# Input projections as seven products for eight, with q, k and v taken through DRAM

## The chip, the core and the metric

The kernel runs on one core of one Trainium2 chip. A core has the matrix engine (PE in the profile, with PEld for its weight loads), the vector engine (DVE), the scalar engine (ACT), GpSimd (POOL) and an engine that here issues nearly all transfers (SP). They run side by side and wait for each other through semaphores. The metric is device time in microseconds of one execution; three runs of the kernel before are shown.

## What is computed

Two layers of a decoder trunk, on 1024 tokens of 1024 columns in f32. Each layer normalises its input, applies gain and shift, and multiplies by one combined weight matrix. Four mLSTM heads and four retention heads of 256 columns work on the result in chunks of the sequence; their gated output is multiplied by a second matrix and added to the input.

```python
for l in range(DEPTH):
    ada = c_act @ w_ada[l] + b_ada[l]
    shift, scale, gate = jnp.split(ada, 3, axis=-1)
    h = rmsnorm(x, norm_g[l]) * (1.0 + scale[:, None, :]) + shift[:, None, :]
    p = h @ w_in[l]
    mq, mk, mv, mo, mz, mi, mf, rq, rk, rv, rz = split_cols(p)
    qk = jax.nn.silu(causal_dwconv(jnp.concatenate([mq, mk], axis=-1), conv_w[l], conv_b[l]))
    ...
    cell = mlstm_chunkwise(mq_c, mk_c, mv, mi + b_igate[l], mf + b_fgate[l])
    y_m = jax.nn.sigmoid(mo) * head_layernorm(cell, gn_m[l], 4) * jax.nn.silu(mz)
    ret = retention_chunkwise(rotary(rq, positions), rotary(rk, positions), rv)
    y_r = head_layernorm(ret, gn_r[l], 4) * jax.nn.silu(rz)
    x = x + gate[:, None, :] * (jnp.concatenate([y_m, y_r], axis=-1) @ w_out[l])
return rmsnorm(x, final_g)
```

The product `h @ w_in[l]` has 1024 rows (tokens), an inner length of 1024 and 9224 columns: q, k, v of eight heads, z of eight heads, o of the four mLSTM heads (1024 columns for each kind and each group of four heads), and eight columns for the input and forget gates.

## The kernel before

**Numbers.** Every f32 operand of a large matmul is split into a high part (ACT casts it to fp32r, L621) and a low part (another engine subtracts, L622; POOL where nothing else is said). `mm3` (L144) makes one product out of three matmuls: high by high, high by low, low by high.

**Tiles.** The normalised input is kept transposed, `hT[k][half]`: eight row tiles `k` of the inner length by two halves of 512 tokens, high and low, 32 tiles of a pool of 62 (`b`). A projection of q, k, z or o takes a block of 128 weight columns as the stationary operand and streams 512 tokens: two halves by eight `k` by three matmuls, 48 matmuls of 512 columns (`proj_units`, L363). The values of a head take 128 tokens as the stationary operand and stream the 256 weight columns: 192 matmuls of 256 columns (`v_path`, L579). PSUM has two pools of four banks: `pp` for projections and `pa` for the rest.

**Order.** PE's order is the program's own: `run_units` (L140) walks a generator of work units, and after each unit `tick` runs the pieces of attention and other side work that are due (`launch`, with a delay in units). The other engines' instructions are put in order by a scheduler at build time; each engine then works strictly in that order. A layer goes: first blocks of z and o of head 0 while the input is being normalised; the values of head 0 together with the eight gate columns (`v0_units`, L434), the rest of head 0's z and o; then for each head z and o blocks, q, k (`qk_ml`, L681, with convolution and SiLU in `conv_silu`, L630; `qk_ret`, L701, with the rotary sums L707 to L717) and v, with the attention of the head before running under them; at last the out projection (`out_units`, L985), whose weights and inputs `OutLoads` (L955) fetches. The mLSTM heads come first (0 to 3), then the retention heads (4 to 7).

**What stays in SBUF.** q and k of a head are split and stay in tiles of pool `b`, v is scaled and split straight out of PSUM (L607, L608). k also goes to DRAM (`kdr`) and back in rows for the state update. The normalised output of a head goes to DRAM (`ndr`, L919), as the gates do (`gdr`).

**Side work.** `rotary_tables` (L374) makes sine and cosine once, under head 1; `ada_columns_later` (L270) makes gain and shift of the second layer under head 4 and after it; `gate_cols` or `gate_rows` (L304, L284) make the gate of the layer from head 5 on.

Of the kernel before, what the change touches and what calls it, by code (L numbers as in the profile page):

```python
# [19 lines left out]
P = 128  # L20
# [15 lines left out]
BIG = 1e30  # L36
WHOLE = (0, 3)
# [43 lines left out]
def tile_hybrid_trunk(ctx, tc, x, xt, c, positions, w_ada, b_ada, norm_g, w_in, conv_w, conv_b,  # L81
# [8 lines left out]
    big = ctx.enter_context(tc.tile_pool(name="big", bufs=62))  # L90
# [53 lines left out]
    def mm3(o, lt, rt, start, stop):  # L144
        PE.matmul(o, lt[0], rt[0], start=start, stop=False)  # L145
        PE.matmul(o, lt[0], rt[1], start=False, stop=False)  # L146
        PE.matmul(o, lt[1], rt[0], start=False, stop=stop)  # L147
# [21 lines left out]
    kdr = [[[dpool.tile([HD, HALF], F32, name=f"kdr{l}_{h}_{i}") for i in range(2)] for h in range(8)]  # L169
           for l in range(DEPTH)]  # L170
# [83 lines left out]
    def ada_rows(l, c0, accs):  # L254
        acc = bt()
        accs.append(acc)
        prev = None
        for k in range(KT + 1):
            raw = None
            if k < KT:  # L260
                raw = wt("raw", 512, 4)
                Q.dma_start(raw, w_ada[l, k * P:(k + 1) * P, c0:c0 + 512])
# [21 lines left out]
    def gate_rows(l, res):  # L284
        for half in range(2):
            accs = []
            yield from ada_rows(l, 2 * D + half * 512, accs)
            brow = wt("th", 512, 5)
# [5 lines left out]
            a2 = (wt("wH", 512, 6, F32R), wt("wL", 512, 6, F32R))  # L294
# [35 lines left out]
    def norm_evac(l, pt, k, on_act=False):  # L330
        hf = wt("acc", 512, 4)
# [16 lines left out]
    def split_w(raw, n, eng=G):  # L348
        wH, wL = wt("wH", 512, 6, F32R), wt("wL", 512, 6, F32R)
# [24 lines left out]
    def rotary_tables():  # L374
        c1, c2, c3 = two_pi_split()
        tiles = [wt("g", 512, 6) for _ in range(3)]
        ang, turn, tmp, rnd, a1, pos = (t[:, i * CH:(i + 1) * CH] for t in tiles for i in range(2))
        a2 = ang
        for n in range(4):
# [13 lines left out]
            for src, cc in ((a1, c2), (a2, c1), (a1, c1)):  # L393
                V.tensor_scalar(tmp, src, cc, None, ALU.mult)
                V.tensor_scalar(rnd, tmp, MAG_I, -MAG_I, ALU.add, ALU.add)
                yield 1
# [16 lines left out]
    def v0_gates(l):  # L413
# [5 lines left out]
    def v0_raw(l, k):  # L419
        raw = wt("raw", 512, 4)[:, 0:HD]  # L420
        Q.dma_start(raw, w_in[l, k * P:(k + 1) * P, OFF_MV:OFF_MV + HD])
        return raw

    def v0_split(gr, raw, k):
        wH, wL = bt(F32R, HD + 8), bt(F32R, HD + 8)
        split_to((wH[:, HD:], wL[:, HD:]), gr[:, k * 8:(k + 1) * 8])
        split_to((wH[:, 0:HD], wL[:, 0:HD]), raw)
        return wH, wL

    def load_v0(l):  # L430
        gr = v0_gates(l)
        return [v0_split(gr, v0_raw(l, k), k) for k in range(KT)]

    def v0_units(l, w, hT, vraw, pgs):  # L434
        g8 = wt("g8", 8 * 36, 1)
        V.memset(g8, 0.0)
        for t in range(8):
            if t % 2 == 0:
                vraw.append(bt())
# [105 lines left out]
    def z_evac(res, m, store=None):  # L545
        def evac(half, pz):
# [5 lines left out]
            if store is not None:  # L552
                Q.dma_start(store[m][half], g)
# [849 lines left out]
```

## Time and profile before

| | us |
|---|---|
| runs (three): median, lowest, highest | 2300.58, 2298.8, 2301.35 |
| profiled execution: span from first to last instruction | 2298.7 |
| out projection of layer 0, about | 1030 to 1170 |
| last out projection, about | 2120 to 2298 |

Times in rows are from the start of the span. A row of a group names the line, the engine, the operation, output and inputs by the program's tile names, shapes and the count, then the summed busy time in us, the mean ns of one, and the idle time of the engine in front of them with what ended most of it. A row of a waits view names the engine and the instruction that waited, what it waited for, us in total, times, and the longest. In a table of stretches each engine has its busy us and its instructions (x), in the order PE, PEld, DVE, ACT, POOL; then the granted clock, the share of the DMA engines and GB/s. Matmuls overlap in the pipe, so the mean ns of a matmul is longer than the distance between two starts.

### The profile page before, as it was taken

The page shows a single profiled execution, that of the slowest core. Times are in us where ns is not written, and L with a number is a line of the kernel's source. Part 1 is how long each engine was busy: PE and PEld are TensorE (multiplying, and loading weights), DVE is VectorE, ACT ScalarE, POOL GpSimd, SP SyncE. Part 2 cuts the span into 40 slices and gives each one's busy share as a digit, 9 for nine tenths or more (in the row PEclk, how much of TensorE's full clock was granted, in tenths as well). Part 3 has the DMA queues.
Part 4 walks back from the last instruction along what each step waited for, and adds up shares of the span by engine and source line. Part 5 has one row for each costly group of instructions (what it writes and reads, how often), then busy time and mean ns, then how long its engine had stood idle before and what let it go on. Part 6 is the DMA issues. An engine that isn't in the chain of part 4 may idle for free. (4 is left out here: it accounts for less than half of the span.)

```text
span 2298.7 us, 34322 instructions
## 1 busy us (share of the span) xinstructions
PE 2269.4 (99%) x12411; PEld 1953.7 (85%) x12411; DVE 1338.7 (58%) x2821; ACT 926.5 (40%) x1785; POOL 827.5 (36%) x820
## 2 busy tenths in 40 slices
PE   7999999999999999999999999999999999999998
PEld 5888888889988888988888889888898898988886
DVE  7467688556555555585435676555564545556563
ACT  7535433444332323343544454444343323234442
POOL 0343333333333334224562434333334334341313
PEclk9999999999999999999999999999999999999999
DMA  8333333324433533476532323233223233436674
GB/s 258 80 69 94 83 80 82 83 70 115 124 110 87 149 96 79 126 254 212 169 105 67 84 71 82 77 77 79 68 71 98 74 91 88 124 84 205 184 242 125
DMA packets 360246, 259.45 MB, mean 113 GB/s; under 512 B 113266, under 2 KB 297338, under 8 KB 360076
## 3 DMA queue, kind: packets, MB, share of 16 engines
q1 hardware_dynamic: 359932, 257.00, 39.8%
q8 instruction: 97, 1.59, 0.3%
q14 instruction: 73, 0.60, 0.1%
q10 hardware_dynamic: 144, 0.26, 0.0%
HBM read 201.57 MB, written 55.61 MB: 112 GB/s over the span
## 5 line engine op out<-in xcount | busy, mean ns | idle before, releaser
L145 PE MATMUL pp<-b,wH 128*128 128x512 f32 x1824 | 719.6, 395 | 0.0
L146 PE MATMUL pp<-b,wH 128*128 128x512 f32 x1824 | 718.6, 394 | 0.0
L147 PE MATMUL pp<-b,wL 128*128 128x512 f32 x1824 | 717.6, 393 | 0.0
L622 POOL TENSOR_TENSOR wL<-raw,wH 128x512 fp32r<-128x512 f32 x338 | 453.9, 1351 | 542.3 <-ACT wH L621 478.7
L147 PEld LDWEIGHTS pp<-b,wL 128*128 128x128 f32 x1824 | 342.5, 188 | 80.4
L145 PEld LDWEIGHTS pp<-b,wH 128*128 128x128 f32 x1824 | 342.7, 188 | 73.1 <-DVE g L550 0.3
L146 PEld LDWEIGHTS pp<-b,wH 128*128 128x128 f32 x1824 | 342.5, 188 | 72.1 <-issue 0.2
L621 ACT CAST wH<-raw 128x512 fp32r<-128x512 f32 x402 | 245.7, 616 | 310.8 <-PE pp L146 109.9
L145 PE MATMUL pp<-wH,b 128*128 128x256 f32 (+1 forms) x1024 | 303.0, 296 | 0.0
L147 PE MATMUL pp<-wH,b 128*128 128x256 f32 (+1 forms) x1024 | 301.9, 295 | 0.0
L146 PE MATMUL pp<-wL,b 128*128 128x256 f32 (+1 forms) x1024 | 301.9, 295 | 0.0
L622 POOL TENSOR_TENSOR b<-acc,b 128x256 fp32r<-128x256 f32 (+1 forms) x192 | 176.6, 939 | 299.0 <-ACT b L621 287.7
L146 PEld LDWEIGHTS pp<-wL,b 128*128 128x128 f32 x1024 | 192.9, 188 | 5.8
L145 PEld LDWEIGHTS pp<-wH,b 128*128 128x128 f32 x1024 | 192.4, 188 | 6.0 <-DVE g L550 0.3
L147 PEld LDWEIGHTS pp<-wH,b 128*128 128x128 f32 x1024 | 192.7, 188 | 5.7
L639 DVE SCALAR_TENSOR_TENSOR acc<-pp,cols,acc 128x511 f32<-128x511 f32 (+2 forms) x192 | 142.4, 742 | 40.7 <-ACT acc L634 38.8
L621 ACT CAST b<-acc 128x256 fp32r<-128x256 f32 (+1 forms) x192 | 83.8, 476 | 180.7 <-DVE acc L716 129.3
L622 POOL TENSOR_TENSOR sL<-th,sH 128x256 fp32r<-128x256 f32 (+1 forms) x62 | 57.9, 934 | 207.7 <-ACT sH L621 161.9
L643 ACT ACTIVATE th<-acc 128x512 f32<-128x512 f32 x64 | 40.5, 632 | 145.7 <-DVE acc L641 77.9
L621 ACT CAST cH<-cf 128x516 fp32r<-128x516 f32 (+1 forms) x80 | 49.8, 622 | 105.8 <-DVE va L903 55.7
L622 DVE TENSOR_TENSOR wL<-raw,wH 128x512 fp32r<-128x512 f32 x64 | 44.3, 694 | 62.5 <-ACT wH L621 58.7
L145 PE MATMUL pa<-b,b 128*128 128x256 f32 (+1 forms) x256 | 72.3, 283 | 1.8 <-DVE th L787 1.0
(297 smaller groups left out, 3639.2 us busy)
## 6 DMA issues: line engine op xcount, KB each, us to landing
raw<-in_w_in_dram SPq DMA_DIRECT2D x274, 256.0 KB
raw<-in_w_out_dram SPq DMA_DIRECT2D x128, 256.0 KB
gdr<-g SPq DMA_DIRECT2D x64, 256.0 KB
ndr<-zt SPq DMA_DIRECT2D x128, 128.0 KB
raw<-in_w_ada_dram SPq DMA_DIRECT2D x64, 256.0 KB
g<-gdr SPq DMA_DIRECT2D x64, 256.0 KB
acc<-ndr SPq DMA_DIRECT2D x64, 256.0 KB
acc<-kdr SPq DMA_DIRECT2D x192, 64.0 KB
```

The costliest lines, as they stand in the source:

```text
L145: PE.matmul(o, lt[0], rt[0], start=start, stop=False)
L146: PE.matmul(o, lt[0], rt[1], start=False, stop=False)
L147: PE.matmul(o, lt[1], rt[0], start=False, stop=stop)
L621: A.copy(dst[0], src)
L622: eng.tensor_tensor(dst[1], src, f(dst[0]), ALU.subtract)
L639: V.scalar_tensor_tensor(acc[:, d:], pt[:, 0:HALF - d], wcol, acc[:, d:], ALU.mult, ALU.add)
L643: A.activation(th, acc, AF.Tanh, scale=0.5)
```

## The change

The weight columns of q, k and z are taken in pairs of 128-column blocks, z and o of an mLSTM head's block as one pair, and the values of two heads as one pair. A pair of column blocks, two halves of the tokens and two halves of the inner length (k tiles 0 to 3 and 4 to 7) make a two by two block product; it is done with seven block products by Strassen's scheme in the form with few additions. Of the input, seven forms of four tiles are kept: three are tiles of `hT` as it is ("11", "21", "22"), four are sums ("T1" to "T4") which `build_forms` makes and splits once a layer. Of the weights, `weight_forms` makes seven forms for a pair; the four additions are on POOL for q and k and on DVE for gates and values, all seven splits on POOL. The products of a pair go to three banks X, Y, Z; some are continued after an intermediate state has been copied out, and `combine` copies (ACT) or adds (DVE) them into the four results, three of which are then tiles in SBUF.

All values of a layer are made ahead of the heads and go to DRAM. q and k of a head go to DRAM when they are made; attention fetches a chunk of each at a time and splits it then. The retention heads come first. The gate columns are a product of their own. The rotary tables are made ahead of the value stage's end; the second layer's columns start after head 5, the gate rows or columns after head 1. The output of a head's attention is stored chunk by chunk, in twice as many transfers. Pools change: `b` 60, `acc` 8, `th` 4, weights 5 tiles each.

```diff
+    def build_forms(hT):
+        F = {"11": [hT[k][0] for k in range(4)], "21": [hT[k][0] for k in range(4, 8)],
+             "22": [hT[k][1] for k in range(4, 8)], "T1": [], "T2": [], "T3": [], "T4": []}
...
+        for k in range(4):
+            t1, b12, b22 = whole(hT[k][0]), whole(hT[k][1]), whole(hT[k + 4][1])
+            V.tensor_tensor(t1, b12, t1, ALU.subtract)
+            V.tensor_tensor(b12, b22, b12, ALU.subtract)
+            V.tensor_tensor(b22, b22, t1, ALU.subtract)
+            keep("T2", b22)
+            keep("T1", t1)
+            keep("T3", b12)
+            t4 = whole(hT[k + 4][0])
+            V.tensor_tensor(t4, t4, b22, ALU.subtract)
+            keep("T4", t4)
+        return F
+
+    ORDER = (("X", "11"), ("Y", "21"), ("X", "T2"), ("Z", "T1"), ("X", "T3"), ("Z", "22"), ("X", "T4"))
+
+    def weight_forms(r11, r12, r21, r22, eng):
...
+        yield split(r11)
+        yield split(r12)
+        eng.tensor_tensor(r21, r21, r22, ALU.add)
+        eng.tensor_tensor(r11, r21, r11, ALU.subtract)
+        yield split(r11)
+        yield split(r21)
+        eng.tensor_tensor(r21, r22, r11, ALU.subtract)
+        yield split(r21)
+        eng.tensor_tensor(r12, r12, r11, ALU.subtract)
+        yield split(r12)
+        yield split(r22)
...
+    def combine(n, bank, keep, done):
+        with tc.high_priority():
+            if n in (0, 2, 3):
+                keep[n] = wt("acc", 512, NACC)
+                A.copy(keep[n], bank["Z" if n == 3 else "X"])
+            elif n < 6:
+                b, m = {1: ("Y", 0), 4: ("X", 3), 5: ("Z", 2)}[n]
+                V.tensor_tensor(keep[m], bank[b], keep[m], ALU.add)
+        if n == 1:
+            done(0, 0, keep[0])
+        elif n == 4:
+            done(1, 1, keep[3])
+        elif n == 5:
+            done(0, 1, keep[2])
+        elif n == 6:
+            done(1, 0, bank["X"])
+
+    def pair_units(feed, F, done):
+        bank, keep = {}, {}
+        for n, (b, form) in enumerate(ORDER):
+            w = feed.take()
+            new = b not in bank
+            if new:
+                bank[b] = ps_p()
+            for k in range(4):
+                mm3(bank[b], w[k], F[form][k], new and k == 0, k == 3, b != "Y")
+            combine(n, bank, keep, done)
+            yield
...
+    def spill(src, l, hg, which, m, half):
+        dst = (kfr if which else qdr)[l][hg][half]
+        Q.dma_start(dst[m * P:(m + 1) * P, :], src)
+        if which:
+            k_store(src, l, hg, m, half)
...
+    def rot_done(l, hg, which, cosT, sinT):
...
+            p0, p1 = got[0, half], got[1, half]
+            s, a, b = wt("acc", 512, NACC), wt("th", 512, NTH), wt("th", 512, NTH)
             V.tensor_tensor(a, p1, sinT[half], ALU.mult)
             V.tensor_tensor(b, p1, cosT[half], ALU.mult)
+            V.tensor_tensor(s, p0, cosT[half], ALU.mult)
+            V.tensor_tensor(p0, p0, sinT[half], ALU.mult)
             V.tensor_tensor(s, s, a, ALU.subtract)
...
+        def fetch_qk(j):
...
+            for dst, dr, tag, bufs in ((qs, qdr, "q", 2), (kx, kfr, "kc", 1)):
+                a = wt("acc", 512, NACC)
+                Q.dma_start(a.rearrange("p (m t) -> p m t", m=2),
+                            dr[l][hg][j // 2].rearrange("(m p) t -> p m t", p=P)[:, :, (j % 2) * CH:(j % 2 + 1) * CH])
+                t = dst[j] = wt(tag, 1024, bufs, F32R)
+                split_to((t[:, 0:512], t[:, 512:1024]), a)
...
+        vh = ((4, 5), (6, 7), (0, 1), (2, 3))
+        heads = (4, 5, 6, 7, 0, 1, 2, 3)
+        gates = [(4, None), (5, None), (6, None), (7, None)] + [(h, m) for h in (1, 2, 3) for m in range(2)]
+        jobs = [("v", p) for p in vh]
+        for i, h in enumerate(heads):
+            if i:
+                jobs.append(("g", gates[i - 1]))
+            jobs += [("qk", (h, 0)), ("qk", (h, 1))]
+        jobs += [("g", g) for g in gates[7:]]
...
+            if which:
+                launch(attention(l, h, gt), 4)
+                if h == 5 and l + 1 < DEPTH:
+                    launch(ada_columns_later(l + 1))
+                if h == 1:
+                    launch(gate_cols(l, gcol) if l == 0 else gate_rows(l, gb))
```

`Feeder.take` asks for weight forms five products ahead. `vpair_units` is `pair_units` for the values of two heads: each product is made for two parts of 256 tokens, 48 matmuls of 256 columns a product and part pair, and the results go to `vdr`. `conv_done` calls `conv_silu` on each result of a q or k pair (for the fourth one after the third), and `spill` behind it; `fetch_kv` fetches a chunk of values and of k rows one chunk ahead.

More of the change, by code (lines that the diff above doesn't have):

```diff
@@ L346, in load_w_raw, with split_w @@
             yield raw
-    def split_w(raw, n, eng=G):
-        wH, wL = wt("wH", 512, 6, F32R), wt("wL", 512, 6, F32R)
+    def split_w(raw, n, eng=G, other=False):
+        wH, wL = (wt(t, 512, b, F32R) for t, b in ((("acc", NACC),) * 2 if other else (("wH", NW), ("wL", NW))))
         split_to((wH, wL), raw, eng)
```

501 lines of the change are left out of this document (258 added, 243 removed), and 4 rows, old and new, of the table script.

## The prediction

> **What bounds the kernel now.** I read the page first, for the share of each engine, then the waits of PE, then the timeline of PE inside a stage.
>
> ```profile
> span 2298.7 us, 34322 instructions
> ...
> PE 2269.4 (99%) x12411; PEld 1953.7 (85%) x12411; DVE 1338.7 (58%) x2821; ACT 926.5 (40%) x1785; POOL 827.5 (36%) x820
> ```
> ```profile
> PE pp L1263 <- DMA b<-in_w_ada_dram: 8.7, 1, 8.7
> PE pp L1204 <- DVE b L1252: 2.8, 2, 1.9
> ...
> PE pa L855 <- DVE cL L622: 2.1, 3, 1.2
> ```
>
> PE is busy throughout. The waits that the trace names for it come to about 20 us, the longest of them in the startup. A busy PE can still issue slowly, so the pace is taken from starts: the first and the last of 24 projection matmuls in a row, and of 59 of the value path; and from the counts of the groups.
>
> ```profile
> 300.46 0.39 PE L145 MATMUL pp<-b,wH 128*128 128x512 f32 x1
> ...
> 305.81 0.39 PE L147 MATMUL pp<-b,wL 128*128 128x512 f32 x1
> ```
> ```profile
> 519.50 0.28 PE L145 MATMUL pp<-wH,b 128*128 128x256 f32 x1
> ...
> 526.35 0.28 PE L146 MATMUL pp<-wL,b 128*128 128x256 f32 x1
> ```
> ```profile
> L145 PE MATMUL pp<-b,wH 128*128 128x512 f32 x1824 | 719.6, 395 | 0.0
> ...
> L145 PE MATMUL pp<-wH,b 128*128 128x256 f32 x896 | 252.4, 282 | 0.0
> ...
> L145 PE MATMUL pp<-b,b 128*128 128x264 f32 x128 | 36.4, 284 | 0.0
> ```
>
> 5.35 us over 23 gaps is 0.2326 us for a 512-wide matmul, 6.85 us over 58 gaps is 0.118 us for a 256-wide one. The mean ns of a row (395, 282) is longer because neighbours overlap. So PE's time is a count of matmuls, and fewer of them shorten the kernel for as long as nothing else becomes late.
>
> **The matmuls removed and added.** In each layer 52 of the 56 column blocks of q, k, z and o are paired. A block takes 48 matmuls of 512, so both layers hold 52 x 48 x 2 = 4992, and seven products for eight remove one in eight: 624 x 0.2326 = 145.1 us. The values are 16 heads x 192 = 3072 matmuls of 256 (2688 in the second group with its two sister lines, 384 of 264 in the third); one in eight is 384 x 0.118 = 45.3 us. The input and forget gates rode on head 0's values at eight more columns, next to nothing; now they take 2 halves x 8 x 3 x 2 layers = 96 matmuls of 512: 22.3 us added. PE alone gives -145.1 - 45.3 + 22.3 = -168 us.
>
> **What the other engines get for it.** The attention now runs under the pairs of q, k and gates only, since all values stand ahead of it. I compare one head's cycle before and after. The windows below are an mLSTM stretch and a retention stretch of layer 1, then the out projections of layer 0 and of layer 1; in each row PE, PEld, DVE, ACT and POOL follow the length.
>
> ```profile
> 1440.00:1570.00 130.00, 130.00 (x724) 112.86 (x723) 72.42 (x167) 53.67 (x107) 46.52 (x49) 1.00 0.29 75
> 1700.00:2000.00 300.00, 300.00 (x1751) 264.08 (x1750) 151.57 (x313) 94.31 (x183) 112.01 (x109) 1.00 0.36 95
> 1030.00:1170.00 140.00, 140.00 (x607) 113.06 (x607) 62.18 (x84) 61.80 (x99) 72.58 (x54) 1.00 0.56 182
> 2120.00:2298.00 178.00, 170.09 (x757) 138.28 (x755) 90.21 (x157) 68.20 (x126) 50.87 (x45) 0.99 0.65 188
> ```
>
> The first row has 724 matmuls; an mLSTM cycle has 8 x 48 + 192 = 576 projection matmuls, which leaves about 140 of attention, 16.5 us. So a cycle was 384 x 0.2326 + 192 x 0.118 + 16.5 = 128.5 us, and by the row it held 71.6 us of DVE and 46.0 of POOL. A retention cycle (6 blocks) was 106.2 us; the second row less 13.9 us of gate rows (L266 below) makes 48.7 us of DVE, and 39.7 of POOL. Afterwards either cycle has two pairs for q and k and about one for gates: 3 x 84 x 0.2326 + 16.5 = 75.1 us of PE.
>
> Prices on DVE and POOL: the group that reads PSUM (L707), one that reads SBUF twice (L622), a convolution tap (L639), the rotary sums (L716, L717), the gate rows; then POOL's splits and ACT's cast.
>
> ```profile
> L707 DVE TENSOR_TENSOR acc<-pp,dm 128x512 f32<-128x512 f32 x32 | 21.8, 681 | 51.6 <-PE pp L147 26.4 <-issue 21.5 <-POOL wL L622 3.7
> L622 DVE TENSOR_TENSOR wL<-raw,wH 128x512 fp32r<-128x512 f32 x64 | 44.3, 694 | 62.5 <-ACT wH L621 58.7 <-PE pa L146 2.1 <-DMA g<-gdr 1.5
> L639 DVE SCALAR_TENSOR_TENSOR acc<-pp,cols,acc 128x511 f32<-128x511 f32 x64 | 47.6, 744 | 38.8 <-ACT acc L634 38.8
> L716 DVE TENSOR_TENSOR acc<-acc,th 128x512 f32<-128x512 f32 x32 | 28.9, 903 | 0.0
> L717 DVE TENSOR_TENSOR acc<-acc,th 128x512 f32<-128x512 f32 x32 | 22.9, 716 | 0.0
> ```
> ```profile
> L266 DVE SCALAR_TENSOR_TENSOR b<-raw,cact,b 128x512 f32<-128x512 f32 x14 | 13.9, 993 | 3.5 <-DMA raw<-in_w_ada_dram 3.4
> ```
> ```profile
> L622 POOL TENSOR_TENSOR wL<-raw,wH 128x512 fp32r<-128x512 f32 x338 | 453.9, 1351 | 542.3 <-ACT wH L621 478.7 <-issue 38.7 <-DMA acc<-kdr 5.7
> L622 POOL TENSOR_TENSOR b<-acc,b 128x256 fp32r<-128x256 f32 x128 | 93.7, 759 | 134.5 <-ACT b L621 134.5
> L622 POOL TENSOR_TENSOR b<-acc,b 128x512 fp32r<-128x512 f32 x64 | 82.8, 1301 | 164.5 <-ACT b L621 153.2 <-DMA acc<-kdr 11.3
> ```
> ```profile
> L621 ACT CAST wH<-raw 128x512 fp32r<-128x512 f32 x402 | 245.7, 616 | 310.8 <-PE pp L146 109.9 <-PE pp L147 58.9 <-DMA raw<-in_w_in_dram 50.7
> ```
>
> DVE, mLSTM cycle: 71.6; less the gating of one pair of z and o of two, four instructions at 0.69, -2.8; nine additions of products from PSUM at 0.68, +6.1; four additions of weights of the gate pair at 0.69, +2.8. That is 77.7 us. Retention: 48.7 + 6.1 + 2.8 = 57.6 (its gating stays). POOL, mLSTM: 20 weight splits become 21, and the q and k pairs add eight additions there: 9 x 1.35 = 12.2; q and k are split when fetched, 8 x 1.30 for 8 x 0.76 + 4 x 1.30 before, -0.9: 57.3 us. Retention: 16 splits become 29: 56.4. ACT gets nine copies of about 0.62 in a cycle on top of 53.0 (53.67 of 130 us, scaled): some 58.5 us of 75, no bound.
>
> So DVE, at 56% of the first window, would be at 77.7 of 75.1 in the mLSTM cycle even if each instruction took as long as before. It won't: more of its instructions read SBUF twice. A convolution read PSUM; now three of four (18 taps of 24 in a cycle) read a sum in SBUF, and so do 12 more rotary instructions and the 8 halves of the values. About 52 in an mLSTM and 50 in a retention cycle have two SBUF inputs. What such an instruction loses to a busier POOL shows in the out projections, where POOL is busy 52% of the time in layer 0 (the third window) and 29% in layer 1 (the fourth). Here the groups of layer 0, then those of layer 1:
>
> ```profile
> L976 DVE SCALAR_TENSOR_TENSOR b<-g,cols,b 128x512 fp32r<-128x512 f32 x16 | 17.4, 1108 | 0.8 <-ACT b L975 0.8
> L622 DVE TENSOR_TENSOR wL<-raw,wH 128x512 fp32r<-128x512 f32 x16 | 11.6, 724 | 17.5 <-ACT wH L621 15.4 <-PE pa L146 2.1
> ...
> L972 DVE TENSOR_TENSOR g<-acc,g 128x512 f32<-128x512 f32 x10 | 7.9, 795 | 3.4 <-DMA g<-gdr 3.3
> ```
> ```profile
> L972 DVE TENSOR_TENSOR g<-acc,g 128x512 f32<-128x512 f32 x23 | 18.3, 815 | 1.5 <-DMA acc<-ndr 1.5
> L976 DVE SCALAR_TENSOR_TENSOR b<-g,cols,b 128x512 fp32r<-128x512 f32 x24 | 18.0, 753 | 8.1 <-ACT b L975 8.1
> L622 DVE TENSOR_TENSOR wL<-raw,wH 128x512 fp32r<-128x512 f32 x23 | 15.6, 684 | 24.4 <-ACT wH L621 24.4
> ```
>
> Over the 42 of layer 0: (16 x 0.355 + 16 x 0.040 - 10 x 0.020) / 42 = +0.15 us each. The ends are nothing and the 0.355 of L976. I take 0.15, the mean of all three groups; afterwards POOL is at 57 of some 80 us, so less is unlikely. The instructions that get a second SBUF input newly pay besides what L716 and L717 pay over the 0.68 of PSUM readers, 0.13 in the mean: 26 x 0.13 = 3.3 and 20 x 0.13 = 2.5. With w for the price, DVE needs 81.0 + 52w in an mLSTM cycle, 60.1 + 50w in a retention one.
>
> Per layer, four mLSTM cycles are over by 4 x (5.9 + 52w); the gate rows or columns add 14; the two further gate pairs at the end (39.1 us of PE, 7.6 each of DVE) take 24 back: 13.6 + 208w. Retention stays under PE for w below 0.30, but in layer 0 the adaLN columns (32 x 0.95 = 30 us) fall on two such heads: 0.2 + 100w. With w = 0.15: 2 x 44.8 + 15.2 = 105 us.
>
> Smaller parts. The forms of the input take 32 DVE and 16 POOL instructions a layer; POOL's share, with the weights due before, is about 26 x 1.35 = 35 us, and the cover (gate matmuls 11.2, the block of o 11.2, two value products 11.3) is 33.7. I take 4 us a layer, 8; without the cover it would be 35 a layer. Rotary tables move from head 1 to the value stage, where DVE is lightly loaded: nothing, or at most their 10 to 20 us once. The out projection is the same but for its order. The spill and fetch of q, k and v I take as hidden; the ends are zero and the DRAM rival below. The sum: -168 + 105 + 8 = -55 us, on the profiled execution's 2298.7 us; the median of the runs shown is 1.9 us above that span. So 2298.7 - 55 + 1.9 = 2246, rounded to 2245.
>
> **Rivals.** *PE stays the bound:* DVE's surplus slips into the value stage and the out projection, where DVE has room (62 of 140 us in the third window), and only the start is lost. 2298.7 - 168 + 8 + 1.9 = 2141. For it: in-order waits of PE on DVE are nearly nil today. Against it: product 3 of a pair accumulates onto the bank that product 1 filled, so PE waits for a copy or addition within one product, 12 x 0.2326 = 2.8 us; DVE can't fall far behind. Those copies stand in ACT's queue behind casts that wait for loads, and their tiles come from the eight that convolutions, fetched tiles and, for a while, the adaLN rows use too; behind a late one stand all later products, since PE goes in order.
>
> *DVE and POOL block each other (slower):* one place, the head stage; one price, w = 0.355 as in the L976 row. Then 27.2 + 416 x 0.355 for the mLSTM cycles, 35.7 for the columns and 2.75 x 6 for the other retention cycles: 227, with the start 235, and 2298.7 - 168 + 235 + 1.9 = 2368. It decides from w = 0.26, where the surplus eats all 168 us. What speaks for it is a stretch where both stand with work:
>
> ```profile
> 1041.59 4.80 DVE L976 SCALAR_TENSOR_TENSOR b<-g,cols,b 128x512 fp32r<-128x512 f32 x3
> ...
> 1044.10 1.74 POOL L1027 TENSOR_TENSOR b<-b,th 128x512 f32<-128x512 f32 x1
> 1045.80 6.86 POOL L622 TENSOR_TENSOR wL<-raw,wH 128x512 fp32r<-128x512 f32 x4
> ```
>
> Three DVE instructions took 4.80 us, each POOL instruction 1.7 us, against 0.75 and 1.30: they alternate. Against it: POOL is seldom ready all the time, it waits for ACT's cast in front of each split. [...]
>
> *The way by DRAM is late:* attention starts four units (11 us) after k's last product and needs scores 8 to 11 us later. In between lie the last two convolutions (three taps of 0.744 and about 1 us more, each: 6.5), the store, the load, a cast and two splits (3.3). An issue on SP, two loads of this size, and what SP waits for most:
>
> ```profile
> 2100.60 0.32 SPq L553
> ...
> 2100.97 4.70 DMA g<-gdr
> ...
> 2106.48 5.40 DMA acc<-ndr
> ```
> ```profile
> SPq L343 <- POOL wL L622: 623.7, 200, 20.9
> ```
>
> That is 6.5 + 4.7 + 5.4 + 3.3 = 20 us of 19 to 22, and attention's own matmuls between the units lengthen the cover: just hidden. The change adds 32 transfers a head (8 spills, 8 fetches of q and k, 4 stores and 4 loads of values, 8 more of the normalised rows); with what is there that makes some 74 issues of 0.32 us in a cycle, 24 us of SP's 75, and about as many bytes again as the 75 to 95 GB/s of the first two windows, at DMA shares of 0.29 and 0.36: room on both. But SP issues in order, and a weight load that waits for its buffer (3.1 us in the mean, 20.9 at most) holds all stores and fetches behind it. If each of 16 heads is late by 10 us on top of the PE bound: 2141 + 160 = 2301.
>
> **How the numbers follow.** Forecast 0.41, PE the bound 0.17, the blocking 0.30, DRAM 0.12. About 0.2% (4.6 us) is what a measurement tells from no change. Faster: 0.38 of the forecast, 0.17, and 0.03 of the DRAM case, 0.58; same 0.05; slower 0.37, of which the blocking is 0.30. The forecast's own range, w from 0 to 0.25, is 2168 to 2297. The range for all reaches down past the PE bound, to 2135, and up to the blocking, 2370; outside lie the worse half of the blocking and some of the PE case.
>
> **What would show it.** Right: PE below 95% in the mLSTM heads with DVE above 90% there, PE waits on DVE or ACT at the product lines, about 11,480 matmuls, two-input DVE groups 0.1 to 0.2 us longer than now. The blocking: these groups at 1.0 us or more, and retention heads short of PE too. DRAM: PE waits at the scores for casts of fetched tiles. Wrong altogether: DVE below 85% in the mLSTM heads while PE stands.

## The result, and the profile after

The changed kernel takes 2891.14 us in the median of four runs, against 2300.69 for the kernel before: the ratio is 1.2568, with a 95% interval of 1.2550 to 1.2585. The forecast was 2245, the range 2135 to 2370. It is not only the size that is wrong but the sign.

The page of the changed kernel, its span and the busy times of the engines:

```profile
span 2889.5 us, 35104 instructions
...
PE 2302.5 (80%) x11483; PEld 1943.4 (67%) x11483; DVE 1826.2 (63%) x3199; ACT 1163.1 (40%) x2149; POOL 1367.5 (47%) x1098
```

The span is 590.8 us longer. PE has 928 matmuls fewer (the 912 to which the prediction's terms add up, and 16 small transposes), and yet is busy 33 us longer. It also stands for 587 us, where it stood for 29. Its waits (engine, what waited, for whom: us in total, times, longest):

```profile
PE pa L896 <- POOL q L743: 126.2, 32, 7.7
PE pa L150 <- ACT kc L742: 123.1, 22, 10.3
PE pa L976 <- ACT cH L742: 59.0, 13, 8.0
PE pp L150 <- ACT wH L742: 44.4, 5, 22.8
PE pa L896 <- POOL kc L743: 43.3, 32, 3.0
PE pp L150 <- ACT acc L646: 38.7, 17, 8.8
PE pa L152 <- POOL kc L743: 33.3, 26, 3.0
...
PE pa L151 <- POOL q L743: 17.6, 18, 3.1
```

Five of these rows are waits of the scores for a fetched q or k, 343 us. The others are spread over the state (cH), the weight forms (wH) and the copies of the banks (acc). One mLSTM cycle shows what the engines do meanwhile. The table by window has the busy time of PE, PEld, DVE, ACT and POOL, and then the granted clock; the window runs from the last store of one head's rows to the last store of the next, 123 us where the prediction had 75 of PE and 89 of DVE:

```profile
2362.30:2485.50 123.20, 85.87 (x383) 70.55 (x381) 90.95 (x182) 54.36 (x107) 63.32 (x54) 0.82 0.40 115
```

No engine is full: PE 70%, DVE 74%, ACT 44%, POOL 51%. The retention heads are no better. A cycle there was to take the 75 us of PE; the one below takes 104, with PE at 80%, DVE at 64% and POOL at 57%, and those of layer 0 take 120 and more:

```profile
1909.70:2014.00 104.30, 83.19 (x392) 69.44 (x391) 66.26 (x114) 37.94 (x73) 59.16 (x48) 0.90 0.41 116
```

A typical stop of PE, from the timeline of the mLSTM cycle above, first PE itself, then ACT, then POOL and DVE (start, duration, and in brackets the idle time and what ended it):

```profile
2404.97 0.39 PE L152 MATMUL pp<-b,wL 128*128 128x512 f32 x1
2411.60 0.58 PE L896 MATMUL pa<-q,kc 128*128 128x256 f32 x1 [6.24 <-POOL q L743]
...
2414.93 0.63 PE L150 MATMUL pp<-b,wH 128*128 128x512 f32 x1
2415.36 0.63 PE L151 MATMUL pp<-b,wH 128*128 128x512 f32 x1
...
2417.46 0.39 PE L150 MATMUL pp<-b,wH 128*128 128x512 f32 x1
2417.69 0.39 PE L151 MATMUL pp<-b,wH 128*128 128x512 f32 x1
```
```profile
2402.74 0.63 ACT L742 CAST cH<-cf 128x516 fp32r<-128x516 f32 x1
2407.78 0.62 ACT L742 CAST wH<-raw 128x512 fp32r<-128x512 f32 x1 [4.42 <-POOL raw L598]
2408.31 0.61 ACT L742 CAST q<-acc 128x512 fp32r<-128x512 f32 x1
```
```profile
2402.92 1.40 POOL L743 TENSOR_TENSOR wL<-raw,wH 128x512 fp32r<-128x512 f32 x1 [3.98 <-ACT wH L742]
2404.28 1.80 POOL L597 TENSOR_TENSOR raw<-raw,raw 128x512 f32<-128x512 f32 x1
2406.16 1.59 POOL L598 TENSOR_TENSOR raw<-raw,raw 128x512 f32<-128x512 f32 x1
2407.83 1.28 POOL L603 TENSOR_TENSOR raw<-raw,raw 128x512 f32<-128x512 f32 x1
2409.05 1.27 POOL L743 TENSOR_TENSOR wL<-raw,wH 128x512 fp32r<-128x512 f32 x1
2410.27 1.27 POOL L743 TENSOR_TENSOR q<-acc,q 128x512 fp32r<-128x512 f32 x1
```
```profile
2404.26 0.68 DVE L743 TENSOR_TENSOR cL<-cf,cH 128x516 fp32r<-128x516 f32 x1
2404.87 0.68 DVE L649 TENSOR_TENSOR acc<-pp,acc 128x512 f32<-128x512 f32 x1
2405.47 1.16 DVE L275 SCALAR_TENSOR_TENSOR acc<-acc,cact,acc 128x512 f32<-128x512 f32 x1
2406.55 0.68 DVE L649 TENSOR_TENSOR acc<-pp,acc 128x512 f32<-128x512 f32 x1
```

Read it from the back. The score at 2411.60 needs the low half of q. POOL makes it at 2410.27, behind two sums, a third, and a split of weights. ACT had stood for 4.42 us at a cast that waits for the second of these sums, with the cast of q behind it in its queue. The sums took 1.80 and 1.59 us and not 1.28, and L275 on DVE took 1.16 and not 0.75 (its median): whether DVE and POOL got in each other's way is tested below. And after the stop PE starts its matmuls 0.43 us apart, and 0.23 apart only from 2417.46 on: the pause also costs clock. The clock records of the trace, 164 stretches, know only half rate (82) and full (82). With a mean granted clock of 0.893, half rate holds for 2 x 0.107 x 2889.5 = 618 us of this run.

### The profile page after: what moved, and what is told of

Same layout as the page of the kernel before. It is cut to its first block, busy times and chain, and to the rows that moved or that the text cites. A ratio compares the mean times of both kernels' runs of the same rounds, so it can differ in the third digit from the quotient of the medians.

```text
span 2889.5 us, 35104 instructions
## 1 busy us (share of the span) xinstructions
PE 2302.5 (80%) x11483; PEld 1943.4 (67%) x11483; DVE 1826.2 (63%) x3199; ACT 1163.1 (40%) x2149; POOL 1367.5 (47%) x1098
## 5 line engine op out<-in xcount | busy, mean ns | idle before, releaser
L743 POOL TENSOR_TENSOR wL<-raw,wH 128x512 fp32r<-128x512 f32 x492 | 674.4, 1378 | 710.8 <-ACT wH L742 655.9
L151 PE MATMUL pp<-b,wH 128*128 128x512 f32 x1616 | 664.1, 411 | 4.2 <-DVE b L1095 4.2
L742 ACT CAST wH<-raw 128x512 fp32r<-128x512 f32 x556 | 340.4, 618 | 633.3 <-PE pp L151 269.8
L151 PEld LDWEIGHTS pp<-b,wH 128*128 128x128 f32 x1616 | 328.6, 203 | 68.9 <-DVE b L1095 5.8
L896 PE MATMUL pa<-q,kc 128*128 128x256 f32 x384 | 105.5, 423 | 169.5 <-POOL q L743 126.2
L150 PE MATMUL pp<-wH,b 128*128 128x256 f32 (+1 forms) x576 | 182.7, 317 | 57.4 <-ACT wH L742 44.4
L649 DVE TENSOR_TENSOR acc<-pp,acc 128x512 f32<-128x512 f32 x180 | 122.4, 681 | 149.6 <-PE pp L152 137.3
L151 PE MATMUL pp<-wL,b 128*128 128x256 f32 (+1 forms) x576 | 182.0, 316 | 13.2 <-POOL wL L743 13.2
L152 PE MATMUL pp<-wH,b 128*128 128x256 f32 (+1 forms) x576 | 181.4, 315 | 0.2
L150 PE MATMUL pa<-wH,b 128*128 128x256 f32 (+1 forms) x576 | 177.1, 307 | 0.0
L151 PE MATMUL pa<-wL,b 128*128 128x256 f32 (+1 forms) x576 | 176.8, 307 | 0.0
L152 PE MATMUL pa<-wH,b 128*128 128x256 f32 (+1 forms) x576 | 176.6, 307 | 0.0
L150 PEld LDWEIGHTS pp<-wH,b 128*128 128x128 f32 x576 | 113.9, 198 | 65.6 <-ACT wH L742 45.4
L754 DVE SCALAR_TENSOR_TENSOR acc<-acc,cols,acc 128x511 f32<-128x511 f32 x144 | 140.3, 974 | 27.2 <-ACT acc L749 26.1
L646 ACT COPY acc<-pp 128x512 f32<-128x512 f32 x180 | 104.2, 579 | 111.8 <-PE pp L152 106.7
L151 PEld LDWEIGHTS pp<-wL,b 128*128 128x128 f32 x576 | 114.0, 198 | 20.4 <-POOL wL L743 15.2
```

The costliest lines, as they stand in the source:

```text
L150: PE.matmul(o, lt[0], rt[0], start=start, stop=False, skip_group_check=more)
L151: PE.matmul(o, lt[0], rt[1], start=False, stop=False, skip_group_check=more)
L152: PE.matmul(o, lt[1], rt[0], start=False, stop=stop, skip_group_check=more)
L646: A.copy(keep[n], bank["Z" if n == 3 else "X"])
L649: V.tensor_tensor(keep[m], bank[b], keep[m], ALU.add)
L742: A.copy(dst[0], src)
```

## The experiments

Eighteen kernels in five groups. Times are medians, each with the 95% interval of its ratio to the kernel before; each was run beside it.

**Is it the short lead of the fetches?** In the changed kernel the fetch of chunk j+2 stands just ahead of the last yield of an iteration, one unit of 2.8 us before the scores that read it.

```
e1_early   scores(j + 1)          + fetch_qk(j + 2, k only)
           values(j, ...)         + fetch_qk(j + 2, q only)
                                  - fetch_qk(j + 2) ahead of finish(j)
e2_dve     - split_to((t[:, 0:512], t[:, 512:1024]), a)
           + split_to((t[:, 0:512], t[:, 512:1024]), a, V)
e3_deep    as e1, kc with 2 buffers, NACC = 6, k fetched for j + 3
e4_plain   blocks by eight plain products, four splits a pair, no forms, no sums
```

> The changed kernel, with the fetch of k of chunk j+2 put directly behind the scores of chunk j+1 (its one buffer comes free there) and the fetch of q of chunk j+2 behind the last values of chunk j (its buffer comes free there): three to four units of projection before the scores that read them, in place of one. Nothing else is moved. Theory A (the fetch has too little lead: one unit of 2.8 us against some 8 to 13 us for load, cast and two splits; and TensorE runs at half rate for a while after each stop): the waits at the scores for fetched q and k, 343 us of the changed kernel, fall under 120 us, the granted clock rises from 0.89 to 0.94 or more, and the time falls from 2891 to 2350 to 2520 us. Theory B (the splits are late because VectorE and GpSimd have too much to do, wherever the fetch stands): the waits stay over 250 us and the time over 2750 us.

> The changed kernel, with the low halves of the fetched q and k (128 subtractions of 128x512, 1.3 to 1.6 us each on GpSimd) made on VectorE in place of GpSimd. Theory A (too little lead): the wait changes its releaser from GpSimd to VectorE or ScalarE and keeps most of its length, since load and cast alone take longer than the one unit of lead; time 2780 to 2900 us. Theory B (the splits stand in GpSimd's queue behind the sums and splits of the weight forms): the 220 us of waits that GpSimd ends go, and with the clock that they cost the time falls to 2550 to 2700 us.

> As the first run, and k with two buffers and fetched right behind the scores of the chunk before, q of chunk 1 fetched with chunk 0; the room comes from the shared scratch tiles, 6 in place of 8. k then has over four units of lead, q three. Theory A: the waits at the scores fall under 60 us, the time 30 to 80 us below the first run, unless six scratch tiles are too few, which would show as waits at the projections for the copies of the banks. Theory B: within 30 us of the first run, both over 2750 us.

> The changed kernel without Strassen's scheme: the same jobs in the same order, the same stores and fetches through DRAM, but each pair by eight plain products (96 matmuls for 84 in the q, k, z, o pairs, 384 for 336 in the value pairs; no forms of the input, four weight splits a pair for seven and no sums of weights). Without a wait TensorE would have some 190 us more to do than the changed kernel has at full clock, which is 2320 to 2350 us. Theory A (lead of the DRAM way, Strassen or not): the scores still wait some 200 to 350 us, clock under 0.95, time 2550 to 2850 us. Theory C (the forms and sums of Strassen's scheme hold up the other engines): the waits go, clock over 0.97, time 2320 to 2400 us.

Measured: e1 2844.3 (1.2328 to 1.2400), e2 2793.9 (1.2110 to 1.2180), e3 2844.1 (1.2327 to 1.2399), e4 2666.9 (1.1559 to 1.1626). In e4 the second token tile of a value bank starts its sum anew, so part of the sums of v is not kept; its instructions are as many as described. The early fetch shortens its own waits, the five rows fall from 343 to 202 us (theory A had asked for under 120, theory B for over 250), but the state's wait grows from 59 to 113:

```profile
PE pa L976 <- ACT cH L742: 112.6, 19, 12.4
PE pa L150 <- ACT kc L742: 71.0, 13, 11.9
PE pa L896 <- POOL q L743: 67.0, 16, 6.8
```

A still earlier fetch (e3) gives nothing more. Lead as the whole cause is refuted. e2 lies in theory A's range, near its lower end, but 128 subtractions taken off POOL give twice as much as the lead that A is about. Plain products with 1008 matmuls more are 224 us faster than Strassen's: what the scheme asks of the other engines costs more than it saves PE. But e4 lies in theory A's range, and it is still 366 us slower than the kernel before: a loss of that size is there with no sum and no saved matmul, in the new order and the way by DRAM. Its scores wait 163 us, less than theory A said.

**Is it the queues, and what stands in them?** A cast of a weight form waits for its buffer (ACT wH <- PE pp L151: 269.8 us in the changed kernel) or for a sum. AHEAD is the number of forms that are made ahead of the one in use: four in the changed kernel.

```
e5_ahead2  - AHEAD = 4
           + AHEAD = 2
e6_nosum   weight_forms: + for r in (r11, r12, r11, r21, r21, r12, r22): yield split(r)
e7_prio    + with tc.high_priority():   around the splits of fetched q, k and of the state
e8_combo   e1, e2 and e5 together
```

> The changed kernel with weight forms made two units ahead in place of four (AHEAD 2 for 4; still five buffers). Theory D: ScalarE's queue, which runs in order, is held by casts of weight forms; the changed kernel shows 270 us in which a cast of wH waits for TensorE's last matmul with the buffer that it is to fill, since with four ahead and five buffers the cast of one form waits for the unit just before, and the casts of q, k and the state stand behind it. Two ahead, the buffer has been free for two units: these 270 us fall under 100, the waits of TensorE fall by 100 us or more, time 2650 to 2780 us. Rival E: what holds ScalarE are the sums of the weights (160 us on GpSimd's L598 and L601, 67 on VectorE's), and forms made later only bring them nearer to their use: the wait moves to the projections (wH, wL at L150 to L152 over 150 us), time 2850 to 3000 us.

> The changed kernel without the sums of weights: the seven forms of a pair are splits of the four loaded pieces, three of them twice (124 sums of 128x512 in two layers of pairs and 64 of value pairs are left out, so the output is not the reference's); casts, splits and matmuls are as many as before. Theory E (casts of weights on ScalarE wait for the sums, and all behind them does): the waits on L597 to L603 go, the time falls by 200 us or more, to 2550 to 2690 us. Theory D (the wait for the buffer): the time falls by less than 100 us, since the casts then wait for the buffers instead.

> The changed kernel with the casts and splits of the fetched q and k and of the state put ahead of other ready work in the order of ScalarE, VectorE and GpSimd; nothing else. If only the order of the queues matters, the waits at the scores and the values (343 and 65 us) fall by half and the time to 2600 to 2750 us. If the order on record already has them as early as their inputs allow and they are held by an instruction that stands waiting in front, little changes: within 60 us of 2891.

> Three edits at once: the fetches of k and q moved ahead as in the run of that kind (alone -47 us), their low halves on VectorE (alone -97 us), and forms two units ahead in place of four. If the three take away different waits, their gains add: 2891 - 47 - 97 - 110 or more (theory D's gain) is 2640 us or less, and under 2550 us if each stall also costs clock. If they are one queue seen from three sides, the time is no lower than the best of them less 40 us.

Measured: e5 2837.8 (1.2307 to 1.2379), e6 2747.5 (1.1915 to 1.1985), e7 2897.1 (1.2564 to 1.2637), e8 2747.3 (1.1914 to 1.1984). The sums that e6 leaves out are 272 (4 x 52 and 64), not the number in its text. The wait for the buffer falls only from 270 to 203 us in e5, where theory D asked for under 100. Another order of the queues alone does nothing. Each thing taken out gives 47 to 144 us, less than its theory asked; and e8 has 144 of the 197 that its three edits gave one by one. None of these waits alone is the cause.

**Does PE's work count at all?**

```
e9_half    - for k in range(4): mm3(...)        in pair_units and vpair_units
           + for k in (0, 3): mm3(...)
e10_once   fetch_qk(j > 0): qs[j], kx[j] = qs[0], kx[0]
e11_all    e8 and e6 together
e12_plain2 e4 with the three edits of e8 and one start of a bank
```

> The changed kernel with half of the projection's matmuls left out of the 26 pairs and 4 value pairs of a layer (of four slices of a form only the first and the last are multiplied); every load, cast, sum, split, copy, store and fetch stays. Left out are 52x42 matmuls at 0.23 us and 8x168 at 0.12, some 660 us of TensorE at full clock. Theory F (in these stages the other engines, passing work to one another in order, set the pace, and TensorE only follows; no engine need be full for it): the time falls by less than 150 us, to 2740 us or more, and the waits of TensorE grow by 450 us or more. Theory G (TensorE's work and a sum of separate short waits make the time): it falls by 400 us or more, to under 2490 us.

> The changed kernel with q and k fetched once a head (chunk 0) and used for all four chunks: three of four fetches, with their casts and splits, are left out, so the output is not the reference's; the scores find their operands ready. Theory A (the 343 us at the scores and the clock that they cost are the loss): the time falls to 2400 to 2500 us. Theory F: what the scores no longer wait for, the state, the copies of the banks and the forms wait for next, and the time falls only by what the left out work lay in the queues, to 2600 to 2750 us.

> The three edits together (fetches early, their low halves on VectorE, forms two ahead; alone 2747 us) and without the sums of weights (alone 2747 us, output not the reference's). If the chain through sums, casts and splits and the chain through the fetches are two separate losses, they add: 2603 us or less. If they are one queue, 2680 us or more.

> The kernel of plain products in the changed order (2667 us), with the same three edits. There are no sums of weights in it and four splits a pair for seven, VectorE 50% and GpSimd 31% busy. If the rest of its loss against the kernel before (some 280 us of idle TensorE and 100 us of clock) is the short lead of the fetches, the time falls to 2420 to 2520 us; if it is the spacing of the attention's steps by units half as long, whatever is fetched, it stays over 2570 us.

Measured: e9 2759.9 (1.1968 to 1.2038), e10 2680.2 (1.1623 to 1.1690), e11 2606.4 (1.1302 to 1.1368), e12 2553.5 (1.1047 to 1.1164). e9 is the sharpest of the early runs. Some 660 us of matmuls gone, 131 us gained, PE's standing up from 587 to 1001 us (414 more, near the 450 of theory F), and the same mLSTM cycle as above is as long as ever:

```profile
2230.60:2355.10 124.50, 63.76 (x266) 49.89 (x266) 97.39 (x182) 56.45 (x110) 63.95 (x55) 0.73 0.43 118
```

PE is busy half of this window and the cycle gets no faster. The whole head stage says the same. These are the stretches from the first head's last store to the eighth's, in both layers, first of the changed kernel, then of e9:

```profile
490.10:1326.70 836.60, 617.30 (x2781) 510.50 (x2780) 565.81 (x1088) 339.77 (x658) 404.93 (x338) 0.85 0.42 120
1909.70:2708.10 798.40, 600.64 (x2718) 495.95 (x2716) 554.35 (x1049) 337.41 (x653) 403.57 (x340) 0.86 0.41 115
```
```profile
445.10:1264.60 819.50, 447.55 (x1918) 361.62 (x1916) 581.63 (x1086) 339.49 (x657) 406.31 (x338) 0.74 0.43 122
1790.60:2574.70 784.10, 448.53 (x1858) 358.50 (x1858) 554.59 (x1045) 335.70 (x651) 408.15 (x340) 0.74 0.42 116
```

1723 matmuls went, 1723 x 0.2326 = 401 us at full clock, and the stretches are 31 us shorter, 1635 to 1604; the other 100 us were gained outside them. In the heads the other engines set the pace, in the cycle above at 78%, 45% and 51%. e10 falls in theory F's range, not in theory A's. e11 points to two separate losses in the chain through the sums and that through the fetches (144 + 144 foreseen, 285 found, 3 us short of its bound); e12 lies between its two expectations.

**Do DVE and POOL exclude each other?** In the trace of the changed kernel, DVE's instructions can be sorted by whether a tensor-tensor instruction of POOL was running when they started. Counts and medians in ns, worked out from every record of a line:

```
line, operands                 two from SBUF   POOL idle     POOL running
L754 acc<-acc,cols,acc              yes        80   742       64   1328
L743 cL<-cf,cH                      yes        60   694       20   1779
L535 acc<-th,acc                    yes        29   690       19   1379
L754 acc<-pp,cols,acc               no         31   734       17    732
L649 acc<-pp,acc                    no         94   683       86    679
L947 cf<-cf,wd,pa                   no         51   475       13    473
L1007 st<-nd                        no         37   419       27    419
```

The same convolution tap (L754) is lengthened when it reads a sum in SBUF (742 to 1328 ns) and not when it reads a bank in PSUM (734 and 732 ns). This lengthening is all that "exclusion", and "lock" in the text of x6, stand for here: no run shows how the two engines share SBUF. Over all DVE instructions, each against the 15th percentile of its own line, tiles and shape, 437 were lengthened by more than 0.15 us, some 365 us together; in the kernel before 199, 140 us.

```
x1_dve        split_to(dst, src, eng=G), split_w(..., eng=G), pair_forms(..., G),
              the scores' split and the second halves of the output weights: G -> V
x2_sums       pair_forms(l, (c, c + P), G): G -> V
x3_dve_early  x1, e1 and e5 together
x4_plain_dve  e12 and x1's edit together
```

> The changed kernel with the splits, and the sums of the weights of q and k, on VectorE in place of GpSimd, which keeps the small powers, the masks and the splits at the change of layer. Theory H (VectorE and GpSimd exclude each other: in the changed kernel 437 of VectorE's instructions take 365 us longer than the same instructions do otherwise, and GpSimd needs about 1.35 us for what VectorE does in 0.69): the lengthening goes (under 80 us), the time falls by 200 us or more, to 2450 to 2690 us, though VectorE then has some 600 us more of its own to do. Theory B' (work queued in order behind other work; it only moves from a queue that is 47% busy to one that is 63% busy): the time rises or stays, 2850 to 3100 us.

> The changed kernel with only the sums of the weights of q and k (128 of 128x512, 1.3 to 1.8 us each) on VectorE in place of GpSimd. Theory H: about half as much as they gave when left out with all others (-144 us), -60 to -110 us, since VectorE needs 0.69 us each and excludes GpSimd meanwhile. Theory C' (only that ScalarE's casts wait for GpSimd's sums, 150 us): the same waits then stand at VectorE's sums, within 40 us of 2891.

> As the run with all splits on VectorE, and the fetches moved ahead and the forms two units ahead in place of four. If the short lead of the fetches and the exclusion are separate losses, this is 60 to 110 us below the run without those two edits, and below 2606 us, the lowest of the kernels with seven products so far; if VectorE alone is now the bound (over 90% busy in the heads), the two edits give less than 30 us.

> The kernel of plain products with fetches ahead, low halves of q and k on VectorE and forms two ahead (2553 us), with all other splits on VectorE too. Theory H: the 117 us by which VectorE's instructions are still lengthened there go, time 2420 to 2500 us, TensorE over 95% busy in the heads. Theory B': within 40 us of 2553.

Measured: x1 2563.6 (1.1112 to 1.1177), x2 2821.0 (1.2228 to 1.2299), x3 2512.1 (1.0889 to 1.0952), x4 2505.5 (1.0860 to 1.0924). x1 is 328 us faster than the changed kernel, though it only gives work to the engine that is busier. The page of x1, and the tap's rows (minimum, median and maximum in ns) in the changed kernel and in x1:

```profile
PE 2220.2 (87%) x11483; PEld 1893.5 (74%) x11483; DVE 1965.8 (77%) x4097; ACT 1168.3 (46%) x2147; POOL 155.6 (6%) x200
```
```profile
L754 DVE SCALAR_TENSOR_TENSOR acc<-acc,cols,acc x144: 700/744/1848, 763.9 to 2603.3; 128x511 f32<-128x511 f32 x48, 128x510 f32<-128x510 f32 x48, 128x509 f32<-128x509 f32 x48
L754 DVE SCALAR_TENSOR_TENSOR acc<-pp,cols,acc x48: 696/734/750, 800.2 to 2599.9; 128x511 f32<-128x511 f32 x16, 128x510 f32<-128x510 f32 x16, 128x509 f32<-128x509 f32 x16
```
```profile
L754 DVE SCALAR_TENSOR_TENSOR acc<-acc,cols,acc x144: 708/742/884, 673.8 to 2288.0; 128x511 f32<-128x511 f32 x48, 128x510 f32<-128x510 f32 x48, 128x509 f32<-128x509 f32 x48
```

898 instructions more cost DVE only 140 us more, mainly since the lengthening falls from 365 to 9 us. The mLSTM cycle is 100 us, and now one engine is nearly full:

```profile
2097.70:2198.10 100.40, 82.30 (x380) 68.98 (x381) 91.81 (x220) 53.56 (x105) 7.26 (x12) 0.86 0.50 142
```

x2 moves 128 sums alone and gains 70 us, inside the range of theory H. But that is hardly the exclusion. Over all records of a trace, a count of the same kind as above gives 357 us of lengthening on DVE in x2 against 363 in the changed kernel, and 120 against 133 on POOL; what changes is that the 128 sums take 122 us on DVE in place of 185 on POOL. So a shorter way through POOL's queue is worth time with the exclusion left nearly as it is. x1 takes away both at once, the exclusion and POOL's slower instructions, and no run separates them: how its 328 us divide stays open.

In x3 lead and AHEAD give another 52 us, a little less than foreseen. In x4 the gain was 48 us; it just misses its range, and PE is 88 to 97% busy in its head cycles, not over 95 throughout. With the splits on DVE, seven products (x3, 2512) and eight (x4, 2506) take the same time within 7 us: the 1008 matmuls saved are worth nothing that these runs can tell. And x4 is still 205 us above the kernel before without any of the scheme's sums, so that much, the gate columns' own product included, belongs to the order and the way by DRAM, which no run takes apart further.

**What is left, and what of the kernel before?**

```
x5_half        x3 with e9's edit
x6_before_dve  kernel before: split_to(dst, src, eng=G), split_w(..., eng=G), scores' split: G -> V
```

> The kernel with all splits on VectorE, fetches ahead and forms two ahead (2512 us), with half of the projection's matmuls left out as in the run of that kind (there -131 us). In its mLSTM heads VectorE is 90% busy and TensorE 85 to 88%. If VectorE's own work now sets the pace there, the time falls by 100 to 200 us; if the chain is broken and TensorE's work counts again, by 300 us or more.

> The kernel before, with its splits of projection weights, fetched tiles and scores on VectorE in place of GpSimd (those of the output stage's second halves and of the change of layer stay). There TensorE is 99% busy and the 140 us by which VectorE's instructions are lengthened lie beside it. If a lock under a covering engine costs nothing, the time stays within 15 us of 2300, and the 140 us fall by more than half; if VectorE, 58% busy, lets the splits come late, it rises by more than 30 us.

Measured: x5 2370.4 (1.0278 to 1.0338), x6 2294.4 (0.9966 to 0.9988). With half the matmuls away x3 falls by 142 us only, in the range of the first answer, and 130 of the 142 lie outside the head stretches, which go from 1330 to 1318 us. In the mLSTM cycles it is DVE's own work, 90% of x3's cycle in the row below, that now sets the pace.

```profile
2147.00:2250.00 103.00, 86.52 (x395) 70.74 (x394) 92.65 (x223) 54.96 (x108) 6.98 (x12) 0.90 0.46 135
```

x6 has the lengthening down from 140 to 19 us, and is 0.23% faster than the kernel before. It is the fastest kernel of this study, faster than both; its page has PE where it was:

```profile
PE 2267.2 (99%) x12411; PEld 1956.3 (85%) x12411; DVE 1501.9 (66%) x3383; ACT 931.9 (41%) x1785; POOL 219.9 (10%) x258
```

## Why the prediction was wrong

**PE's work.** The count was right (11,483 for "about 11,480"; the terms shown give 11,499, without the 16 transposes), and with it the 168 us at full clock. But the sum then carried the saved work over to the time, less DVE's surplus. Run e9 shows that in the head stage PE's work has hardly a price: 401 us of it went and 31 us were gained. The **clock** was left out of the sum altogether: 2269.4 - 168 = 2101 us were expected of PE, 2302.5 were found, 201 us more. By the clock records 382 us of PE's busy time ran at half rate, which is 191 of the 201. The kernel before stood for 29 us, and its records show full rate from 21 us after its start to 4 us before its end. In the trace of the changed kernel half rate comes with the stops: the one shown above lasts 6.2 us, and half rate holds until 5.9 us after the restart. From its first clock record on, of the 28 stops of 0.3 to 1 us that began at full rate 1 ended at half rate, and of those over 5 us all 27; 81 of the 82 half-rate stretches in the records last a whole multiple of 3.41 us.

**The step that failed** is the one that takes a cycle as long as its busiest engine: "DVE needs 81.0 + 52w in an mLSTM cycle", 88.8 us against PE's 75.1, so 13.7 us over. The cycle took 123 with DVE at 74%. That is the last sign on the list, under "wrong altogether". The needs themselves were near, DVE 91.0, ACT 54.4 and POOL 63.3 us where 88.8, 58.5 and 57.3 were foreseen; for DVE that is partly luck, since its lengthening was larger than the term for it (below) and the rest smaller. It was the step from the largest need to the length of the cycle that failed, and in the retention cycles too, with 104 to 131 us for 75. What stands in its place: a result passes from POOL's sum to ACT's cast to POOL's split to PE, in queues that run in order, so that what waits holds all behind it (in the stop above ACT's cast of q behind 4.42 us), and no engine need be full. With POOL nearly taken out of this chain (x1, 7.3 us of POOL in the cycle) the cycle is 100 us, 9% over DVE's need. Two things in it made POOL dear, its instructions of 1.3 us and more (1378 ns in the mean for the 492 splits of loaded weights), and the time that DVE and POOL take from each other (365 us of lengthening on DVE, 133 on POOL); x2 points to a price of the first by itself, and the share of the second is not shown. The 89 of DVE would have been right only for engines that work independently.

**w, the price of the exclusion**, was 0.15 for 816 instructions with two SBUF inputs, 122 us. The lengthening grew by 365 - 140 = 225, that is 0.28 if it all falls on those 816: the term took little more than half of it, and 0.28 is beyond the point of 0.26 from which the prediction itself let the blocking decide. The mean over the out projection's groups was too low a row; the change makes POOL busy for half of the time (51% in the mLSTM cycle above) just where DVE's convolutions no longer read PSUM. But even the rival with 0.355, which had the sign and the place right, and a lengthening that is there, came to only 2368: it too priced DVE's own lengthening alone, and not what POOL loses, nor ACT behind POOL, nor the clock. In the sorted table the instructions with two SBUF inputs take 690 to 742 ns with POOL idle and 1328 to 1779 with POOL running; the others keep their time (the largest difference is 4 ns, 683 to 679).

**The way by DRAM** was "just hidden". That sum looked at a head's first chunk, which has 19 to 22 us of cover. Chunks 2 and 3 are fetched one unit ahead. The sign named for it, PE waiting at the scores for casts of fetched tiles, is the largest group of waits (343 us, 21 a head, where that rival had 10). Its price is smaller than its row: fetched once, -211 us with all the work that this spares; earlier alone, -47; on top of x1, and with AHEAD, -52. So a wait at the end of a shared queue was not worth its length here.

**What was right:** the count of matmuls, POOL's need in an mLSTM cycle (57.3 us, 63.3 found with its own lengthening), PE's waits at the products (38.7 us on ACT's copies; only 7.4 on DVE's additions), and that the other engines could make this end slower. **What stays open:** how much of the loss the exclusion is, and the last 211 us of x3. DVE at 90% and x5 put the mLSTM heads down to DVE's work; but x4, with the plain products, is as slow with DVE 61% busy, which points to the order and the way by DRAM. Nor was it tried to bring the sums or low halves to an engine other than these two.

## What to carry to other kernels

Before trading matmuls for additions, follow an added instruction through the queues that its result passes, not engine by engine, and look where its operands lie: a result copied from PSUM to SBUF gives its later readers on DVE a second SBUF input, and those are the ones that were lengthened here while POOL ran (the convolution tap from 742 to 1328 ns). When PE stands and nobody is full, take PE's work away: if the time of the stage stays, the saved matmuls are worth nothing there. And a split that POOL makes in 1.3 us and DVE in 0.69 belonged on DVE here, as long as DVE had room, and cost nothing even where PE is 99% busy (x6, 2294.4 us for 2299.5).

## What was unexpected of the hardware

Half of 618 us at half rate is some 310 us of lost rate, of which 191 us fell on busy time. In e9 and x5, where PE has least to do, the mean clock is lowest, 0.796 and 0.844 (0.893 in the changed kernel, 0.946 in x3), so that part of what fewer matmuls save is given back by slower ones. And moving 562 instructions in x6 to the busier engine made a kernel faster whose PE was already 99% busy; 2.2 of the 6.5 us by which its span is shorter (2298.7 to 2292.2) are PE's own busy time.
